# Four output projection tiles of eight by Strassen's block products in a two-layer hybrid decoder trunk

## The chip, the cores and the metric

The kernel runs on one core of a Trainium2 chip. The core has five engines that run programs of their own and meet at semaphores: TensorE (PE in the profile; its weight loads are listed as PEld), VectorE (DVE), ScalarE (ACT), GpSimd (POOL) and SyncE (SP), which issues nearly all DMAs here. Every engine takes its instructions in order. Matmuls read SBUF and write PSUM, of which this kernel uses eight banks of 128 x 512 float32. The metric is the time of one execution on the device in microseconds, median of the runs shown.

## The reference

512 tokens and 16 meta tokens in front of them (528 columns) pass through two layers with a residual stream of 1024 features, all float32. Cut to what matters:

```
for l in range(2):
    h = rmsnorm(h_res, norm_gain[l])
    u_pool, z_pool, c_q, c_kv, k_rope, z_mla, g_pool, g_mla = split(h @ w_in[l])
    y_pool = (pool_mix(u_pool, ...) * pool_scale * silu(z_pool)) @ pool_w_up[l]
    o_mla  = mla(c_q, c_kv, k_rope, ...)               # latent attention, 8 heads
    y_mla  = (o_mla * silu(z_mla)) @ mla_w_up[l]
    merged = sigmoid(g_pool) * y_pool + sigmoid(g_mla) * y_mla
    h_res  = h_res + merged @ w_out[l]                 # 1024 x 1024
return h_res[:, 16:]
```

The change is in the last line of the loop, `merged @ w_out[l]`.

## The kernel before

**Layout.** Activations lie transposed: a tile is 128 features by 528 tokens. In the second layer most work, and the output projection with it, is for the 512 real tokens alone (`self.x0` is 0 in the first layer, 16 in the last).

**Matmuls.** Each float32 operand is split into a high part, rounded to the type of the fast matmul, and a low part, the rest. `mm3` (L180) issues three matmuls: high weight by high data (L181), high weight by low data (L182), low weight by high data (L183). The weight of a step is 128 x 512 (four blocks of 128 in the contraction) and comes through `wload`: SyncE loads `raw`, ScalarE copies it to the high part `whi` (L176), VectorE subtracts to get the low part `wlo` (L177). Loads run four steps ahead of use. Data is split the same way by `split` (L274): ScalarE writes the high part (L275), VectorE the low one (L276).

**Order.** All large products stand in one list, `plan`, which the generator `stream` walks; between its steps the program of the layer (`go`) places the attention and the elementwise work. `upto` advances the stream to a named product, `fill_now` by some time of an internal clock, `after` puts a function off by such a time, and `flush` runs all that was put off. A scheduler then orders each engine's instructions by its own estimate, so the order on an engine differs from the order in the text where two instructions don't depend on each other.

**Around the change.** After the gates come the eight products `mu0` to `mu7` (contraction 512). For each, `ev_mu` multiplies the PSUM result by the gate on VectorE (L980), adds the pooled branch `am` on GpSimd into the scratch buffer `tmp` (L982; `am` is held in `xb`), and splits the sum into `mg[m]` (the names `hh` and `hl` in the profile, since the tiles lie in the buffers of the normalised input). Then come the eight output tiles `o0` to `o7`, contraction 1024, two weights each. In the first layer a tile is two halves of 264 columns, 48 matmuls of 264; in the second one half of 512, 24 matmuls, except `o7`, which has two of 256. In the first layer, where `o0` and `o1` begin, the stream puts the first weight of `o1` ahead of the second of `o0`. `ev_o` adds half of the PSUM result to the residual on VectorE (L996; the factor belongs to the gates) and stores it: to `scr` in the first layer, where the new residual stays in `xb` too and is squared and split for the next layer (L342), to the output `yT` in the second.

**Buffers.** `tmp` has three buffers, `raw` three, `whi` and `wlo` three each, the spare pair `th` and `tl` two each. PSUM has four banks `mm`, three `S` and one `o`.

Of the kernel before, what the change touches and what calls it, by code (L numbers as in the profile page):

```python
# [9 lines left out]
F32 = mybir.dt.float32  # L10
F32R = mybir.dt.float32r
# [44 lines left out]
SPL = 240  # L56
RET = 12500.0
WARM = 8


def cut(v, bits):
# [10 lines left out]
def trunk(ctx, tc, xT, xrow, mrow, pos, win, wkr, wqb, wkb, wvb, wgr, wpu, wmu, wout, gains, const, yT):  # L72
# [89 lines left out]
    class Gemm:  # L162
        def __init__(self, name, src, width, evac=None, xs=None, segs=None, body=None):
            self.name, self.src, self.width, self.alloc = name, src, width, mmt
            self.evac, self.xs, self.segs, self.body = evac, xs, segs, body
            self.spare = False

    loads = [0]

    def wload(src, n, spare):  # L170
        raw = early.pop(0) if early else fetch(src, n, rawt(), sp)
        loads[0] += 1
        pool, th, tl, nb = (tp, "th", "tl", 2) if loads[0] <= 2 or spare else (wp, "whi", "wlo", 3)
        hi = pool.tile([P, W if pool is tp else 512], F32R, tag=th, name=nm("whi"), bufs=nb)
        lo = pool.tile([P, W if pool is tp else 512], F32R, tag=tl, name=nm("wlo"), bufs=nb)
        act.activation(hi[:, :n], raw[:, :n], AF.Copy)  # L176
        dve.tensor_sub(lo[:, :n], raw[:, :n], hi[:, :n].bitcast(F32))  # L177
        return hi, lo

    def mm3(out, wh, wl, xh, xl, start, stop):  # L180
        first = pe.matmul(out, wh, xh, start=start, stop=False)  # L181
# [8 lines left out]
    def stream():  # L190
        flat = [(g_, c) for g_ in plan for c in range(0, g_.width, 512)]
        names = [g_.name for g_, c in flat]
        for i in (1, names.index((0, "o0")) + 1):
            flat[i], flat[i + 1] = flat[i + 1], flat[i]

        def load(i):
            g_, c = flat[i]
            n = min(512, g_.width - c)
# [48 lines left out]
    def after(ns, fn):  # L247
        pend.append((clk[0] + ns, fn))
        pend.sort(key=lambda e: e[0])
# [19 lines left out]
    def fill_now(ns):  # L269
        end = clk[0] + ns  # L270
        while clk[0] < end and step():
            pass

    def split(hi, lo, src, a, b):  # L274
        act.activation(hi[:, a:b], src, AF.Copy)  # L275
        return dve.tensor_sub(lo[:, a:b], src, hi[:, a:b].bitcast(F32))  # L276
# [40 lines left out]
    class Layer:  # L317
        def __init__(self, l):
            self.l, self.last = l, l == DEPTH - 1
            self.XS = XTOK if self.last else FULL  # L320
            self.x0 = NM if self.last else 0
            self.xt = xt if l == 0 else [None] * 8
            self.hs, self.us, self.zps = hbuf, [None] * 4, [None] * 4
            self.cs, self.cqs, self.ys, self.am = [None] * 2, [None] * 6, [None] * 4, [None] * 8
            self.kn, self.qn, self.zms, self.ogs = [None] * 4, [None] * 4, [None] * 4, [None] * 4
            self.qr, self.qf = [None] * 2, [None] * 2
            self.gms, self.mg, self.xr, self.vw = [None] * 8, [None] * 8, [None] * 8, []
            self.made = [None] * 8
            self.csq, self.xsq = [None] * 2, [None] * 8
            self.sq = []  # L330
            self.hosted = self.st = self.acc = self.inv = self.cinv = self.kraw = self.kp = None

        def g(self, c):
            return gn[:, self.l * N_GAIN + c:self.l * N_GAIN + c + 1]
# [640 lines left out]
        def ev_mu(self, m):  # L975
            def ev(ps, a, b):
                if a == self.x0:
                    self.mg[m] = self.hs[m]
                t = tmp()
                dve.scalar_tensor_tensor(out=t[:, :b - a], in0=self.gms[m][:, a:b], scalar=1.0, in1=ps,  # L980
                                         op0=ALU.add, op1=ALU.mult)
                gp.tensor_add(t[:, :b - a], t[:, :b - a], self.am[m][:, a:b])  # L982
# [24 lines left out]
        def register(self, nxt):  # L1007
# [4 lines left out]
            def add(name, src, width, **kw):  # L1012
                plan.append(Gemm((l, name), src, width, **kw))
# [59 lines left out]
        def go(self, nxt):  # L1073
# [58 lines left out]
            if not self.last:  # L1132
                for p in range(4):
                    self.meta_out(p)
            up("o7")
            if nxt is not None:
                for k in range(8):
# [79 lines left out]
```

## Time and profile before

| | |
|---|---|
| median of 3 runs | 770.41 us (770.23 to 770.59) |
| profiled execution, span from the first to the last instruction | 768.5 us |
| TensorE busy | 763.8 us, 99% |
| VectorE busy | 544.1 us, 71% |
| ScalarE busy | 408.9 us, 53% |
| GpSimd busy | 201.6 us, 26% |
| granted TensorE clock | 1.00 |

The profile is of one execution; what the runs' time has beyond its span, 1.9 us, lies before the first and after the last instruction. A row of the timeline gives the start in us from the span's start, the duration in us, the engine, the line of the kernel, the operation, output and inputs by the program's names, and shapes; `xN` joins N of them in a row. A row of groups gives, after the count, the union of busy time in us, the mean duration of one in ns, and the idle time of the engine ahead of them with what ended it. Durations of neighbouring instructions overlap, since each begins while the one before drains; what one costs on an engine that is full is the distance of their starts. A wait for several semaphores is put down to the one that came last.

### The profile page before, as it was taken

The page shows a single profiled execution, that of the slowest core. Times are in us where ns is not written, and L with a number is a line of the kernel's source. Part 1 is how long each engine was busy: PE and PEld are TensorE (multiplying, and loading weights), DVE is VectorE, ACT ScalarE, POOL GpSimd, SP SyncE. Part 2 cuts the span into 40 slices and gives each one's busy share as a digit, 9 for nine tenths or more (in the row PEclk, how much of TensorE's full clock was granted, in tenths as well). Part 3 has the DMA queues.
Part 4 walks back from the last instruction along what each step waited for, and adds up shares of the span by engine and source line. Part 5 has one row for each costly group of instructions (what it writes and reads, how often), then busy time and mean ns, then how long its engine had stood idle before and what let it go on. Part 6 is the DMA issues. An engine that isn't in the chain of part 4 may idle for free.

```text
span 768.5 us, 14355 instructions
## 1 busy us (share of the span) xinstructions
PE 763.8 (99%) x5195; PEld 697.9 (91%) x5195; DVE 544.1 (71%) x1179; ACT 408.9 (53%) x892; POOL 201.6 (26%) x251
## 2 busy tenths in 40 slices
PE   9999999999999999999999999999999999999998
PEld 9999999999999999999997898887888888888887
DVE  5588687357899977785376486773677989775842
ACT  6755656545556665634264355454446666664320
POOL 2026204012242233052220262040132434420500
PEclk9999999999999999999999999999999999999999
DMA  8533233343223222325642333334433332222372
GB/s 293 160 113 98 75 97 98 104 141 105 89 79 91 84 71 70 107 71 169 178 133 97 110 86 89 96 87 127 125 119 90 94 93 77 82 69 70 119 222 98
DMA packets 54931, 84.05 MB, mean 109 GB/s; under 512 B 10006, under 2 KB 18582, under 8 KB 54860
## 3 DMA queue, kind: packets, MB, share of 16 engines
q1 hardware_dynamic: 54716, 82.87, 35.6%
q8 instruction: 41, 0.67, 0.4%
q14 instruction: 30, 0.25, 0.1%
q10 hardware_dynamic: 144, 0.26, 0.1%
HBM read 76.69 MB, written 4.29 MB: 105 GB/s over the span
## 4 chain that ended last, share of the span: by engine, by line
PE 99%; DMA 0%; ACT 0%; DVE 0%; SPq 0%; issue 0%; ACTq 0%
PE mm L181 29%; PE mm L183 29%; PE mm L182 29%; PE mm L859 2%; PE S L181 2%; PE S L182 2%; PE S L183 2%; PE o L876 1%; PE o L872 1%; PE S L503 1%; PE S L470 0%; DMA xb<-xT 0%; PE S L806 0%; PE mm L922 0%; PE mm L395 0%; PE S L872 0%
## 5 line engine op out<-in xcount | busy, mean ns | idle before, releaser
L181 PE MATMUL mm<-hh,whi 128*128 128x264 f32 (+2 forms) x1080 | 339.9, 317 | 0.0
L182 PE MATMUL mm<-hl,whi 128*128 128x264 f32 (+2 forms) x1080 | 338.2, 314 | 0.0
L183 PE MATMUL mm<-hh,wlo 128*128 128x264 f32 (+2 forms) x1080 | 337.1, 315 | 0.0
L177 DVE TENSOR_TENSOR wlo<-raw,whi 128x512 fp32r<-128x512 f32 (+2 forms) x251 | 186.7, 748 | 98.6 <-ACT whi L176 94.6
L176 ACT ACTIVATE whi<-raw 128x512 fp32r<-128x512 f32 (+2 forms) x251 | 150.2, 602 | 181.3 <-PE mm L182 135.3
L181 PEld LDWEIGHTS mm<-hh,whi 128*128 128x128 f32 x1080 | 202.5, 188 | 12.9 <-ACT kp L474 0.4
L182 PEld LDWEIGHTS mm<-hl,whi 128*128 128x128 f32 x1080 | 203.0, 188 | 12.2
L183 PEld LDWEIGHTS mm<-hh,wlo 128*128 128x128 f32 x1080 | 201.9, 188 | 12.2
L743 POOL TENSOR_TENSOR tmp<-kp,bc 64x528 f32<-64x528 f32 x16 | 25.6, 1600 | 123.9 <-PE mm L183 70.0
L604 POOL TENSOR_TENSOR racc<-racc,tmp 128x264 f32<-128x264 f32 (+1 forms) x15 | 14.3, 956 | 133.1 <-ACT tmp L603 133.1
L832 POOL TENSOR_TENSOR pm<-pa,rs 128x16 f32<-128x16 f32 x32 | 9.1, 285 | 126.1 <-DVE rs L827 126.1
L982 POOL TENSOR_TENSOR tmp<-tmp,xb 128x264 f32<-128x264 f32 (+1 forms) x24 | 26.9, 1138 | 56.0 <-DVE tmp L980 55.9
L774 DVE CUSTOM_DVE_ANT_0 S<-S,maskw,nqs 128x400 f32<-128x400 f32 (+4 forms) x80 | 38.4, 499 | 4.4 <-PE S L183 4.0
L781 ACT ACTIVATE cq<-S,bia 128x400 f32<-128x400 f32 (+2 forms) x48 | 24.6, 516 | 27.1 <-DVE bia L774 18.1
L181 PE MATMUL mm<-u,whi 128*128 128x264 f32 (+1 forms) x108 | 34.7, 322 | 0.0
L181 PE MATMUL mm<-cq,whi 128*128 128x264 f32 (+1 forms) x108 | 34.7, 321 | 0.0
L183 PE MATMUL mm<-u,wlo 128*128 128x264 f32 (+1 forms) x108 | 34.7, 321 | 0.0
L183 PE MATMUL mm<-cq,wlo 128*128 128x264 f32 (+1 forms) x108 | 34.5, 321 | 0.0
L182 PE MATMUL mm<-cq,whi 128*128 128x264 f32 (+1 forms) x108 | 34.5, 321 | 0.0
L834 POOL TENSOR_TENSOR cq<-cq,rs 128x384 f32<-128x384 f32 (+1 forms) x32 | 32.8, 1024 | 0.0
L276 DVE TENSOR_TENSOR tl<-mm,th 128x384 fp32r<-128x384 f32 (+1 forms) x48 | 27.9, 596 | 5.0 <-ACT th L275 4.8
L275 ACT ACTIVATE th<-mm 128x384 fp32r<-128x384 f32 (+1 forms) x48 | 24.1, 523 | 10.2 <-PE mm L859 9.2
(270 smaller groups left out, 1378.6 us busy)
## 6 DMA issues: line engine op xcount, KB each, us to landing
raw<-win SPq DMA_DIRECT2D x143, 256.0 KB, 2.6
raw<-wout SPq DMA_DIRECT2D x32, 256.0 KB, 3.0
bc<-kdr SPq DMA_DIRECT2D x16, 264.0 KB, 3.6
raw<-wpu SPq DMA_DIRECT2D x16, 256.0 KB, 2.7
raw<-wmu SPq DMA_DIRECT2D x16, 256.0 KB, 2.7
raw<-wqb SPq DMA_DIRECT2D x12, 256.0 KB, 2.6
xb<-xT SPq DMA_DIRECT2D x8, 264.0 KB, 5.7
tmp<-xT SPq DMA_DIRECT2D x16, 132.0 KB, 3.4
```

Source lines behind the costliest of these rows:

```text
L176: act.activation(hi[:, :n], raw[:, :n], AF.Copy)
L177: dve.tensor_sub(lo[:, :n], raw[:, :n], hi[:, :n].bitcast(F32))
L181: first = pe.matmul(out, wh, xh, start=start, stop=False)
L182: pe.matmul(out, wh, xl, start=False, stop=False)
L183: newest[0] = pe.matmul(out, wl, xh, start=False, stop=stop)
L275: act.activation(hi[:, a:b], src, AF.Copy)
L276: return dve.tensor_sub(lo[:, a:b], src, hi[:, a:b].bitcast(F32))
L743: gp.tensor_mul(kf[r0:r0 + 64, :], self.kp[r0:r0 + 64, :], bc[r0:r0 + 64, :])]
L774: return dve.tensor_tensor_reduce(out=sv, in0=sv, in1=mask, scale=nqs[:, i, h:h + 1], scalar=3e38, op0=ALU.add, op1=ALU.min, accum_out=bia ...
L781: act.activation(pv, sv, AF.Exp, scale=-1.0, bias=bia[:, i:i + 1], accum_out=rs[:, c:c + 1])
L834: gp.tensor_mul(pt[i][:, NM:], pt[i][:, NM:], rs[:, i:i + 1].to_broadcast([P, n - NM]))
L982: gp.tensor_add(t[:, :b - a], t[:, :b - a], self.am[m][:, a:b])
```

## The change

`o4` to `o7` become two pairs, (4, 5) and (6, 7). A pair is a product of a 256 x 1024 weight with 1024 x 528 (or 512) data. Cut in halves in all three directions it is a 2 x 2 block product: eight block products in the plain way, seven in Strassen's (here in Winograd's form). A block product is 12 matmuls: four blocks of 128 in the contraction, three matmuls each, over half the tokens (`HV`: 264 columns in the first layer, 256 in the second).

- **Sums of data.** With `lo` and `hi` the `merged` values of the feature tiles 0 to 3 and 4 to 7, and a and b the two halves of the tokens, `combine` makes four sums for each of four tiles on VectorE: `lo_a - lo_b`, that `+ hi_b`, `hi_b - lo_b`, and the second `- hi_a`. The first and third kind follow `ev_mu` by `LAG`, the others come in `combine_split`, which splits each sum into high (ScalarE) and low (VectorE), at a distance of `PACE` after `mu7`. To keep the unsplit values, GpSimd's addition in `ev_mu` now writes `am` itself in place of `tmp`.
- **Sums of weights.** `weight_sums` loads the four 128 x 512 weights of a pair into free buffers by SyncE, each behind the newest matmul at that place, and GpSimd adds: s1 = a21 + a22, s2 = s1 + a11, a21 becomes a11 + a21, and, when the fourth operand is asked for, a12 becomes s2 + a12. (All are sums since the second tile of a pair is computed with its sign turned, which the factor -0.5 at the residual turns back.) The loads are the same in number and size as before, but bypass `raw` and its three buffers.
- **Products.** `pair_body` runs the seven. Three PSUM banks are used, and sums over products are formed in PSUM: a bank goes on accumulating after VectorE has added its state at that time to the residual (`add`, with factor 0.5 or -0.5). So VectorE reads a bank seven times per pair, and products 2, 4 and 6 follow on a bank that was just read. The residual rows of both tiles are loaded whole at the start.
- `wload`'s splitting becomes `parts`, which the pairs use on the seven weight operands (seven splits per pair where four loads were split before).
- In the second layer `o7` loses its own two halves, since the pairs have halves anyway.

```diff
+PAIRS = (2, 3)
+PACE = 300.0
...
-                gp.tensor_add(t[:, :b - a], t[:, :b - a], self.am[m][:, a:b])
-                split(*self.mg[m], t[:, :b - a], a, b)
+                f = self.am[m][:, a:b]
+                gp.tensor_add(f, t[:, :b - a], f)
+                split(*self.mg[m], f, a, b)
+                if b == T:
+                    after(LAG, lambda: self.combine(1 if m < 4 else 3, m % 4))
...
+        def combine(self, w, k):
+            f = self.tf[w, k] = sqt()[:, :n]
+            if w == 1:
+                eng.tensor_sub(f, lo[:, a0:b0], lo[:, a1:b1])
+            elif w == 2:
+                eng.tensor_add(f, hi[:, a1:b1], self.tf[1, k])
+            elif w == 3:
+                eng.tensor_sub(f, hi[:, a1:b1], lo[:, a1:b1])
+            else:
+                eng.tensor_sub(f, self.tf[2, k], hi[:, a0:b0])
+
+        def combine_split(self, w, k):
+            if w in (2, 4):
+                self.combine(w, k)
...
+            sign = -1.0 if w == 2 else 1.0
+            act.activation(th, f, AF.Copy, scale=sign)
+            dve.scalar_tensor_tensor(out=tl, in0=f, scalar=sign, in1=th.bitcast(F32), op0=ALU.mult, op1=ALU.subtract)
+
+        def weight_sums(self, p):
...
+                behind(sp.dma_start(t[m, c], wout[self.l, 2 * p + m, :, c:c + 512]), newest[0])
+            self.ws[p] = [a11, a12, s2, s1, a21, a12, a22]
+            for d, x, y in ((s1, a21, a22), (s2, s1, a11), (a21, a11, a21)):
+                fill_now(LAG if p > PAIRS[0] else 300)
+                gp.tensor_add(d, x, y)
+
+        def pair_operand(self, p):
+            def operand(i):
+                if i == 3:
+                    gp.tensor_add(ops[1], ops[2], ops[1])
+                return parts(ops[i], 512, i % 2 == 1, dve)
...
+                if i == 0:
+                    product(B, w, quarter(0, a0, b0), True)
+                    add(m1, a0, b0, B, 0.5, False)
+                elif i == 1:
+                    product(A, w, quarter(4, a0, b0), True)
+                    add(m1, a0, b0, A, 0.5, True)
+                elif i == 2:
+                    product(B, w, ts(2), False)
+                    add(m1, a1, b1, B, 0.5, False)
+                elif i == 3:
+                    product(C, w, ts(1), True)
+                    add(m2, a1, b1, C, -0.5, False)
+                elif i == 4:
+                    product(B, w, ts(3), False)
+                    add(m2, a1, b1, B, -0.5, True)
+                elif i == 5:
+                    product(C, w, quarter(4, a1, b1), False)
+                    add(m1, a1, b1, C, 0.5, True)
+                else:
+                    product(B, w, ts(4), False)
+                    add(m2, a0, b0, B, -0.5, True)
...
-            for m in range(8):
-                add(f"o{m}", wout[l, m], D, evac=self.ev_o(m, nxt), xs=mg,
-                    segs=[(NM, NM + SEQ // 2), (NM + SEQ // 2, T)] if self.last and m == 7 else XS)
+            for m in range(2 * PAIRS[0]):
+                add(f"o{m}", wout[l, m], D, evac=self.ev_o(m, nxt), xs=mg, segs=XS)
...
+            for p in PAIRS:
+                add(f"o{2 * p + 1}", None, 7 * 512, body=self.pair_body(p, nxt))
+                plan[-1].operand = self.pair_operand(p)
...
+            up("mu7")
+            flush()
+            self.weight_sums(PAIRS[0])
+            for w in (2, 1, 3, 4):
+                for k in range(4):
+                    fill_now(PACE)
+                    self.combine_split(w, k)
+            for p in PAIRS[1:]:
+                self.weight_sums(p)
             up("o7")
```

More of the change, by code (lines that the diff above doesn't have):

```diff
@@ L165, in __init__, with parts @@
             self.evac, self.xs, self.segs, self.body = evac, xs, segs, body
-            self.spare = False
+            self.spare, self.operand = False, None
     loads = [0]
+    def parts(raw, n, spare, eng):
+        pool, th, tl, nb = (tp, "th", "tl", 2) if spare else (wp, "whi", "wlo", 3)
+        hi = pool.tile([P, W if pool is tp else 512], F32R, tag=th, name=nm("whi"), bufs=nb)
+        lo = pool.tile([P, W if pool is tp else 512], F32R, tag=tl, name=nm("wlo"), bufs=nb)
+        act.activation(hi[:, :n], raw[:, :n], AF.Copy)
+        eng.tensor_sub(lo[:, :n], raw[:, :n], hi[:, :n].bitcast(F32))
+        return hi, lo
     def wload(src, n, spare):
@@ L172, in wload @@
         loads[0] += 1
[L173 to L178, printed above, removed]
+        return parts(raw, n, loads[0] <= 2 or spare, dve)
     def mm3(out, wh, wl, xh, xl, start, stop):
@@ L197, in load @@
             g_, c = flat[i]
+            if g_.operand is not None:
+                return g_.operand(c // 512)
             n = min(512, g_.width - c)
@@ L331, in __init__ @@
             self.hosted = self.st = self.acc = self.inv = self.cinv = self.kraw = self.kp = None
+            n = (T - self.x0) // 2
+            self.HV = [(self.x0, self.x0 + n), (self.x0 + n, T)]
+            self.tf, self.ts, self.ws = {}, {}, {}
         def g(self, c):
@@ new lines, in weight_sums @@
+        def weight_sums(self, p):
+            tags = (("cq0", "cq1", "cq2", "cq3", "kn0", "kn1"), ("q0", "q1", "q2", "q3", "kn2", "racc"))[p % 2]
+            t = {}
+            for tag, (m, c) in zip(tags, ((0, 0), (0, 512), (1, 0), (1, 512))):
+                t[m, c] = slot(tag)[:, 0:512]
+                behind(sp.dma_start(t[m, c], wout[self.l, 2 * p + m, :, c:c + 512]), newest[0])
+            a11, a12, a21, a22 = (t[k] for k in ((0, 0), (0, 512), (1, 0), (1, 512)))
+            s1, s2 = (slot(tag)[:, 0:512] for tag in tags[4:])
+            self.ws[p] = [a11, a12, s2, s1, a21, a12, a22]
+            for d, x, y in ((s1, a21, a22), (s2, s1, a11), (a21, a11, a21)):
+                fill_now(LAG if p > PAIRS[0] else 300)
+                gp.tensor_add(d, x, y)
@@ L1134, in go @@
                     self.meta_out(p)
+            up("mu7")
+            flush()
+            self.weight_sums(PAIRS[0])
+            for w in (2, 1, 3, 4):
+                for k in range(4):
+                    fill_now(PACE)
+                    self.combine_split(w, k)
+            for p in PAIRS[1:]:
+                self.weight_sums(p)
             up("o7")
```

51 lines of the change are left out of this document (added).

## The prediction

> **What bounds the kernel now.** First the page's busy times and the chain of work that ended last:
>
> ```profile
> PE 763.8 (99%) x5195; PEld 697.9 (91%) x5195; DVE 544.1 (71%) x1179; ACT 408.9 (53%) x892; POOL 201.6 (26%) x251
> PE 99%; DMA 0%; ACT 0%; DVE 0%; SPq 0%; issue 0%; ACTq 0%
> ```
>
> TensorE is busy for 763.8 of 768.5 us, and 99% of the chain is TensorE: a matmul fewer is time won, as long as nothing makes TensorE wait. So the question is what a matmul costs, and how close the other engines already are where the change adds work to them. Prices of matmuls, from the timeline of TensorE (start, duration; the durations overlap, the pace is start to start):
>
> ```profile
> 351.93 0.28 PE L181 MATMUL mm<-hh,whi 128*128 128x264 f32 x1
> 353.39 0.28 PE L181 MATMUL mm<-hh,whi 128*128 128x264 f32 x1
> 730.83 0.39 PE L181 MATMUL mm<-hh,whi 128*128 128x512 f32 x1
> 737.76 0.39 PE L181 MATMUL mm<-hh,whi 128*128 128x512 f32 x1
> 759.25 0.28 PE L181 MATMUL mm<-hh,whi 128*128 128x256 f32 x1
> 760.67 0.28 PE L181 MATMUL mm<-hh,whi 128*128 128x256 f32 x1
> ```
>
> The first two rows are 12 matmuls apart, the next two 30, the last two 12: 0.122 us for 264 columns, 0.231 for 512, 0.118 for 256.
>
> Next the stretch in which the `mu` tiles are evicted, just ahead of the output projection, once per layer (columns: span of the stretch, then busy us of PE, PEld, DVE, ACT, POOL):
>
> ```profile
> 329.42:351.63 22.21, 22.21 (x184) 22.21 (x183) 20.73 (x38) 10.54 (x23) 14.58 (x16) 1.00 0.27 78
> 708.07:728.55 20.48, 20.48 (x90) 16.57 (x89) 19.38 (x24) 9.56 (x16) 12.29 (x8) 1.00 0.30 92
> 731.00:765.00 34.00, 34.00 (x171) 28.52 (x170) 11.65 (x19) 6.32 (x10) 0.00 (x0) 1.00 0.53 164
> ```
>
> VectorE's 71% is a mean. In both `mu` stretches it is at 93 to 95%, while in the projection itself it is at a third. The groups of those two stretches (count, busy us, mean ns, idle before) show what it does there:
>
> ```profile
> L276 DVE TENSOR_TENSOR hl<-tmp,hh 128x264 fp32r<-128x264 f32 x16 | 11.3, 720 | 1.2 <-ACT hh L275 1.2
> L177 DVE TENSOR_TENSOR wlo<-raw,whi 128x512 fp32r<-128x512 f32 x6 | 4.8, 819 | 0.0
> L980 DVE SCALAR_TENSOR_TENSOR tmp<-cq,mm 128x264 f32<-128x264 f32 x12 | 4.8, 421 | 3.2 <-PE mm L183 3.0
> ...
> L177 DVE TENSOR_TENSOR wlo<-raw,whi 128x512 fp32r<-128x512 f32 x8 | 8.8, 1117 | 0.0
> L276 DVE TENSOR_TENSOR hl<-tmp,hh 128x512 fp32r<-128x512 f32 x8 | 7.1, 905 | 1.1 <-ACT hh L275 1.1
> ```
>
> The subtraction L276 has the same width as the eviction L980, and takes 720 ns to its 421. The timeline says why:
>
> ```profile
> 343.40 0.76 DVE L980 SCALAR_TENSOR_TENSOR tmp<-cq,S 128x264 f32<-128x264 f32 x2
> 343.96 2.58 POOL L982 TENSOR_TENSOR tmp<-tmp,xb 128x264 f32<-128x264 f32 x3 [1.12 <-DVE tmp L980]
> 344.08 0.93 DVE L276 TENSOR_TENSOR hl<-tmp,hh 128x264 fp32r<-128x264 f32 x1
> ```
>
> Two evictions take 0.76 us together, 0.34 from one to the next; a subtraction that begins while GpSimd adds needs 0.93 alone. Operations with two SBUF inputs wait for GpSimd's and the other way round; those that read PSUM don't. So VectorE and GpSimd together are nearly full here.
>
> **What is saved.** Per layer the change replaces four tiles by 2 x 7 products of 12 matmuls, 168 in all. In the first layer they replace 192 of the same width: 24 x 0.122 = 2.9 us. In the second they are 256 wide and replace three tiles of 24 at 512 and one of 48 at 256: 72 x 0.231 + 48 x 0.118 - 168 x 0.118 = 2.5. Together 5.4 us, all on the path.
>
> **What is added to VectorE.** Per layer 16 token sums and 16 splits of a half row (0.34 each; the 256 columns of the second layer are priced the same), 14 evictions for 8 (for 5 in layer two), and the weight splits 14 for 8. In the projection this has room. But in the changed kernel's order on VectorE, 12 sums and 7 splits of them stand ahead of the last split of `mg7`, which every output tile needs: 19 x 0.34 = 6.5 us. Nothing shows that they hide: they have two SBUF inputs, like L276. They can use the idle time that the groups show, 1.2 and 1.1.
>
> First layer: `mg7` is split here:
>
> ```profile
> 351.20 0.43 DVE L276 TENSOR_TENSOR hl<-tmp,hh 128x264 fp32r<-128x264 f32 x1 [0.20 <-ACT hh L275]
> 354.62 0.29 PE L182 MATMUL mm<-hl,whi 128*128 128x264 f32 x1
> ```
>
> It ends at 351.63 and TensorE reads it at 354.62, a margin of 3.0. TensorE's order up to that matmul holds the same work in both kernels, so it waits 6.5 - 1.2 - 3.0 = 2.3 us. After that VectorE has 3 weight splits (0.6 each) and 9 short ones up to the low part of `o2`'s first weights, 4.9 us, against 41 matmuls, 5.0: the wait neither grows nor shrinks.
>
> Second layer: the last split ends at 728.55, and here one more weight split stands ahead of it (0.6), so it comes 6.5 + 0.6 - 1.1 = 6.0 later, at 734.5:
>
> ```profile
> 727.87 0.68 DVE L276 TENSOR_TENSOR hl<-tmp,hh 128x512 fp32r<-128x512 f32 x1
> 720.38 0.39 PE L181 MATMUL mm<-hh,whi 128*128 128x512 f32 x1
> ```
>
> TensorE begins `o0` at 720.38 and has 46 matmuls of 512 and 10 of 256 (part of the first product, moved up) before it needs it: 720.4 + 10.6 + 1.2 = 732.2, a wait of 2.4. Then VectorE has 3 weight splits, 10 short ones and two evictions (3 x 0.6 + 10 x 0.34 + 2 x 0.6 = 6.4) up to the low part of `o2`'s second weights, TensorE only 20 matmuls (4.4): 2.0 more, 4.4 in all.
>
> **GpSimd's sums of weights**, four per pair, 512 wide. The nearest row of that width that nobody holds up:
>
> ```profile
> L604 POOL TENSOR_TENSOR racc<-racc,tmp 128x512 f32<-128x512 f32 x5 | 6.5, 1292 | 68.4 <-ACT tmp L603 68.4
> ```
>
> Three of them, 3.9 us, follow the `mu` additions directly, so they fall on those late splits of VectorE. If they land beside evictions or waits they cost 0, if they hold VectorE up for their whole time 3.9 per layer; I take the middle, 2.0 and 1.9. The Trainium skill (SBUF — State Buffer, "Who interferes with whom") says that the shared pair of ports is held for the whole instruction and the other engine blocks fully: by that it would be the upper end, and the time about 3.9 us more than I forecast; the 0.93 us row agrees with the rule, but not that every sum must meet a split.
>
> **Loads and banks.** The parts' weights are as many loads as before, but in the second layer SyncE's order has pair 3's four behind a store of `yT` that waits for pair 2's first finished half.
>
> ```profile
> raw<-wout SPq DMA_DIRECT2D x32, 256.0 KB, 3.0
> 764.81 0.28 PE L183 MATMUL mm<-hh,wlo 128*128 128x256 f32 x1
> 765.13 0.42 DVE L996 SCALAR_TENSOR_TENSOR tmp<-mm,tmp 128x256 f32<-128x256 f32 x1 [0.99 <-PE mm L183]
> ```
>
> Some 3 us for the first and perhaps 1 each for the others (an estimate), then up to four sums of 1.3 and a split: 13 us, against the 105 matmuls of 256, 12.4 us, that stand between; only the operand made last is that late. Bounds 0 and 2, I take 0.5. Products of one bank follow each other with other work between, except the last two of the second layer: there TensorE waits from its last start (764.81 in the old end) until the eviction is over, 0.7 us. The residual rows and stores are the same bytes. ScalarE gets 16 short copies and 6 weight copies more per layer; at 10.5 of 22 us it has room, so I take 0. The end (a 256-wide eviction and its store) stays.
>
> **Sum.** -5.4 + (2.3 + 2.0) + (4.4 + 1.9) + 0.5 + 0.7 = +6.4 us, made on an execution of 768.5 us span; the runs' median is 770.4, 1.9 more, which the change leaves as it is. Forecast 776.8. With no GpSimd hold and no late load: -5.4 + 2.3 + 4.4 + 0.7 = +2.0, 772.4. With both whole: -5.4 + 6.2 + 8.3 + 2.7 = +11.8, 782.2.
>
> **Rivals.** (1) Faster: the lateness hides. Of VectorE's time 16 x (720 - 420) + 6 x (819 - 680) ns = 5.6 us in the first stretch is waiting for GpSimd (680 is a 512-wide subtraction unhindered, the 727.87 row), in the second 8 x 437 + 8 x 225 = 5.3. The change lets GpSimd write its sum in place, which frees the three `tmp` buffers sooner; if GpSimd then runs beside the evictions, 5.6 + 1.2 pays for 6.5. It decides when VectorE regains some 5 us per layer. Then only the bank wait is left: 765.7. Against it: GpSimd needs some 0.86 us for each of 16 additions (2.58 for the three above) and the 16 evictions offer 0.34 of cover each. Chance 0.17. (2) Half of that: waits about equal the saving, 769 to 772.3, chance 0.09; 0.2% (1.5 us) is about what a measurement of this kernel can tell from no change, and 0.08 lies within it. (3) The clock. Every stretch above has a granted clock of 1.00, with no wait of microseconds in it; the new waits are the first. Were the clock halved for some 3.4 us after each of the two, 1.7 us each would be lost: 780.2, chance 0.08. The Trainium skill (TensorE: Matmul & The Clock Gate, "What's actually happening") has that rule, half rate after an idle window of about 3.4 us; no run so far shows it, and the waits are broken up by matmuls. The forecast itself has 0.66.
>
> **The range** 765.6 to 782.5 holds rival 1's value and the upper bound; some 0.08 lies below and 0.08 above. The forecast's own range is 772.4 to 782.2. Faster 0.17, the same 0.08, slower 0.75.
>
> **What would show it.** In the new profile: TensorE idle by some microseconds between the last `mu` tile and `o2` in both layers, released by VectorE (`hl`, then `wlo`); VectorE over 95% there; 264- and 256-wide products at 0.122 and 0.118; the new sums at 0.7 or more where GpSimd runs; no idle time inside the products except the last bank. I am wrong if TensorE stays gapless at `mg7`: then rival 1 holds and 5 us are gained.

## The result, and the profile after

The changed kernel takes 796.16 us (median of 4 runs, 794.90 to 797.41) against 770.5 for the kernel before on the same chip: a ratio of 1.0333, 95% interval 1.0318 to 1.0348. It is slower by 25.7 us; the forecast was 776.8 with a range to 782.5. The profiled execution took 797.41 us with a span of 795.6, 27.1 more than the span before.

The busy times and the chain of the changed kernel:

```profile
PE 771.6 (97%) x5219; PEld 703.6 (88%) x5219; DVE 591.0 (74%) x1270; ACT 426.5 (54%) x936; POOL 223.6 (28%) x267
...
PE 88%; DVE 7%; DMA 2%; issue 1%; POOL 0%; ACT 0%; SPq 0%; DVEq 0%; ACTq 0%
```

Before, 99% of the chain was TensorE; now 7% of the way to the end runs over VectorE and 2% over transfers. What TensorE waits for in the whole execution, the six largest rows (total us, times, longest):

```profile
PE mm L187 <- DVE hl L283: 5.5, 4, 2.9
PE mm L1062 <- DVE tmp L1068: 3.9, 3, 3.0
PE mm L1062 <- ACT whi L176: 2.8, 1, 2.8
PE mm L186 <- DVE tmp L990: 2.1, 2, 1.9
PE S L1062 <- ACT whi L176: 1.5, 2, 0.9
PE S L1062 <- DVE wlo L177: 1.4, 1, 1.4
```

Line 283 is `mg`'s split, 990 the eviction of the `mu` tiles, 1068 the eviction of the products, 176 and 177 the split of weights. None of these rows stood in the old profile. Where they lie, in stretches of 5 us (columns: us; busy time of TensorE, its weight loads, VectorE, ScalarE and GpSimd with instruction counts; granted clock; DMA share; GB/s):

```profile
345.00:350.00 5.00, 4.01 (x33) 3.80 (x31) 5.00 (x10) 2.02 (x6) 2.55 (x3) 1.00 0.17 62
350.00:355.00 5.00, 4.05 (x20) 4.05 (x21) 5.00 (x11) 1.80 (x5) 2.63 (x3) 0.66 0.31 91
355.00:360.00 5.00, 5.00 (x43) 5.00 (x42) 5.00 (x10) 3.29 (x8) 2.50 (x4) 1.00 0.75 255
360.00:365.00 5.00, 2.10 (x17) 1.88 (x16) 5.00 (x7) 2.31 (x5) 3.63 (x3) 1.00 0.01 2
...
380.00:385.00 5.00, 4.10 (x33) 3.76 (x31) 1.88 (x3) 1.69 (x3) 3.24 (x3) 1.00 0.83 267
385.00:390.00 5.00, 2.52 (x18) 2.35 (x19) 4.35 (x9) 2.32 (x4) 4.11 (x3) 1.00 0.63 187
...
740.00:745.00 5.00, 3.11 (x12) 1.64 (x10) 5.00 (x5) 2.71 (x6) 3.72 (x4) 1.00 0.71 236
745.00:750.00 5.00, 2.76 (x10) 2.06 (x11) 5.00 (x8) 1.86 (x6) 2.96 (x2) 0.74 0.00 0
750.00:755.00 5.00, 5.00 (x17) 4.19 (x16) 5.00 (x14) 2.94 (x8) 0.00 (x0) 0.58 0.19 52
...
770.00:775.00 5.00, 2.29 (x20) 2.08 (x18) 0.42 (x1) 0.54 (x1) 0.00 (x0) 0.97 0.78 233
775.00:780.00 5.00, 4.24 (x18) 3.95 (x19) 2.21 (x5) 1.42 (x4) 2.67 (x3) 0.50 0.48 157
```

Three things are to be seen. VectorE is busy the whole time from 345 to 365 and from 740 to 755 while TensorE is not. At 380 to 390 and 770 to 775 VectorE is not full and the DMA engines are busy for 0.63 to 0.83 of the time: these waits are for transfers, as the rows below show. And behind several stops the clock column drops (0.66, 0.74 and 0.58, 0.50): TensorE is busy and slow.

The 27.1 us, from the trace: for every matmul the time to the start of the next, less the usual one of its shape, added up by place.

| term | forecast | measured |
|---|---|---|
| saving of the products | -5.4 | -5.5 |
| first layer, `mu` to `o2` | 2.3 + 2.0 | 6.1 of waits (2.10, 3.06, 0.97), 1.6 of slow clock |
| first layer, residual rows of the pairs | 0 | 3.7 (3.13, 0.57) |
| second layer, `mu` to `o3` | 4.4 + 1.9 | 6.3 of waits (seven, the longest 1.93), 3.2 of slow clock |
| second layer, pair 3's loads | 0.5 | 5.0 of waits (3.01 the longest), 2.3 of slow clock |
| last bank | 0.7 | 0.7 |
| the start | 0 | 1.9 |
| the tail, and gaps under 0.3 | 0 | 1.8 |

The start: in the stretch from 5 to 10 us TensorE got 36 matmuls done before and 21 in the changed kernel's profiled execution, although the granted clock is shown as 1.00 in both. From 5.98 to 9.94 its matmuls start at twice their usual spacing, which costs 1.86 us.

```profile
5.00:10.00 5.00, 4.91 (x36) 4.68 (x37) 4.02 (x8) 3.55 (x7) 0.00 (x0) 1.00 0.99 317
```

```profile
5.00:10.00 5.00, 4.81 (x21) 4.69 (x22) 3.40 (x7) 3.50 (x7) 0.00 (x0) 1.00 0.94 307
```

The first row is of the kernel before, the second of the changed one. The four runs of the changed kernel fall into two pairs 2.3 us apart; the profile is of the upper pair.

**The first layer's stop at 360.** The timeline of the changed kernel has VectorE's four sums of line 1008 (two SBUF inputs) beside GpSimd's first weight sum:

```profile
357.98 3.63 DVE L1008 TENSOR_TENSOR sq<-xb,sq 128x264 f32<-128x264 f32 x4
...
358.45 1.45 POOL L1037 TENSOR_TENSOR kn<-cq,cq 128x512 f32<-128x512 f32 x1 [1.72 <-DMA cq<-wout]
```

Four sums take 3.63 us; at 0.34 from one to the next they would take 1.4. The first eviction of `mu0` and the last split of `mg7` are these:

```profile
331.34 1.11 DVE L990 SCALAR_TENSOR_TENSOR tmp<-cq,mm 128x264 f32<-128x264 f32 x3 [2.92 <-PE mm L188]
...
362.97 0.42 DVE L283 TENSOR_TENSOR hl<-xb,hh 128x264 fp32r<-128x264 f32 x1
```

The split ends 32.05 us after the eviction began, in the kernel before 22.21: 9.8 us later. 6.5 of it is the price of the 19 new operations, and 3.3 come from GpSimd's three weight sums, as the run without them shows below; none of the old idle time came back. TensorE had a margin of 3.0 us, so it must come 6.8 us late to that split, and it does: 2.10 us of stop at a `mu` eviction, 1.6 of slow clock and 3.06 of stop at the split. The slow clock adds nothing here: at full speed TensorE would have stood 1.6 us longer at the split.

**The residual rows.** The longest wait of VectorE from 370 to 392:

```profile
DVE xb L1126 <- DMA tmp<-xT: 4.9, 2, 4.4
```

And SyncE's issues in that time (start us, us, line, transfer):

```profile
374.91 1.43 SPq L1031 DMA_DIRECT2D q<-wout  x3
376.38 0.45 SPq L1123 DMA_DIRECT2D tmp<-xT  x1
...
377.35 2.04 SPq L1123 DMA_DIRECT2D tmp<-xT  x2
...
382.76 0.38 SPq L1086 DMA_DIRECT2D tmp<-xT  x1
...
385.69 0.38 SPq L1086 DMA_DIRECT2D tmp<-xT  x1
```

The rows of the last output tile (line 1123) are issued behind pair 3's weight loads (line 1031) and share the transfers with them; VectorE stands 4.4 us at that tile's eviction. The pair's own rows (line 1086) go into `tmp`, which has three buffers, and each waits for such an eviction and its store to free one. So the first product's eviction has its row only after 386, and TensorE waits for the bank.

**Pair 3's loads.** The chain from 765 to 777 (start us, us, what):

```profile
765.98 2.98 DMA yT<-tmp
...
768.97 0.32 SPq L1086
...
769.82 0.42 SPq L1031
...
770.29 5.55 DMA q<-wout
...
775.87 0.64 ACT whi L176
```

SyncE cannot issue the load of a residual row (line 1086) until a store has freed its `tmp` buffer, and pair 3's four weight loads (line 1031) stand behind it in SyncE's order. They are issued from 769.82 on, when pair 2 has some 2 us of matmuls left. The first weight has landed at 774.36, behind the stop of 3.01 us, and the second, 5.55 us under way, at 775.84, behind the stop of 0.91.

### The profile page after: what moved, and what is told of

Same layout as the page of the kernel before. It is cut to its first block, busy times and chain, and to the rows that moved or that the text cites. A ratio compares the mean times of both kernels' runs of the same rounds, so it can differ in the third digit from the quotient of the medians.

```text
span 795.6 us, 14545 instructions
## 1 busy us (share of the span) xinstructions
PE 771.6 (97%) x5219; PEld 703.6 (88%) x5219; DVE 591.0 (74%) x1270; ACT 426.5 (54%) x936; POOL 223.6 (28%) x267
## 4 chain that ended last, share of the span: by engine, by line
PE 88%; DVE 7%; DMA 2%; issue 1%; POOL 0%; ACT 0%; SPq 0%; DVEq 0%; ACTq 0%
PE mm L186 24%; PE mm L188 24%; PE mm L187 24%; PE mm L1062 3%; PE mm L869 2%; DVE wlo L177 2%; PE S L186 2%; PE S L188 2%; PE S L187 2%; DVE hl L283 1%; PE o L886 1%; PE o L882 1%; DVE tmp L990 1%; DMA tmp<-xT 1%; PE S L513 1%
## 5 line engine op out<-in xcount | busy, mean ns | idle before, releaser
L187 PE MATMUL mm<-hl,whi 128*128 128x264 f32 (+1 forms) x976 | 308.8, 317 | 5.5 <-DVE hl L283 5.5
L186 PE MATMUL mm<-hh,whi 128*128 128x264 f32 (+1 forms) x976 | 309.8, 319 | 2.1 <-DVE tmp L990 2.1
L188 PE MATMUL mm<-hh,wlo 128*128 128x264 f32 (+1 forms) x976 | 306.7, 318 | 0.0
L177 DVE TENSOR_TENSOR wlo<-raw,whi 128x512 fp32r<-128x512 f32 (+2 forms) x235 | 175.8, 751 | 79.1 <-ACT whi L176 75.4
L176 ACT ACTIVATE whi<-raw 128x512 fp32r<-128x512 f32 (+2 forms) x235 | 140.0, 600 | 142.5 <-PE mm L187 92.2
L187 PEld LDWEIGHTS mm<-hl,whi 128*128 128x128 f32 x976 | 185.1, 190 | 18.2 <-DVE hl L283 7.4
L186 PEld LDWEIGHTS mm<-hh,whi 128*128 128x128 f32 x976 | 184.8, 190 | 14.4 <-DVE tmp L990 2.8
L188 PEld LDWEIGHTS mm<-hh,wlo 128*128 128x128 f32 x976 | 184.0, 190 | 11.6 <-DVE wlo L177 0.6
L993 POOL TENSOR_TENSOR xb<-tmp,xb 128x264 f32<-128x264 f32 (+1 forms) x24 | 26.8, 1137 | 63.2 <-DVE tmp L990 63.2
```

Source lines behind the costliest of these rows:

```text
L177: eng.tensor_sub(lo[:, :n], raw[:, :n], hi[:, :n].bitcast(F32))
L187: pe.matmul(out, wh, xl, start=False, stop=False)
L188: newest[0] = pe.matmul(out, wl, xh, start=False, stop=stop)
L993: gp.tensor_add(f, t[:, :b - a], f)
```

## The experiments

Theory A, after the trace: the products save what was forecast, and the loss is made of four things that can be taken away one by one: data sums on VectorE ahead of `mg7`, GpSimd's weight sums that hold VectorE up, transfers issued late, and the slow clock behind every stop. Theory B: VectorE, GpSimd and the loads are simply too full there, so what is moved comes back elsewhere.

**No data sums.** The `after(LAG, combine)` and the splits are gone, and the products read quarters of `mg` in their place.

```diff
-                if b == T:
-                    after(LAG, lambda: self.combine(1 if m < 4 else 3, m % 4))
...
-                ts = lambda w_: [self.ts[w_, k] for k in range(4)]
+                ts = lambda w_: quarter(4 * (w_ % 2), a0, b0)
...
-                    self.combine_split(w, k)
```

> The data sums and their splits are left out (the three products that read them read quarters of the merged data in their place, so the output is not the reference's); all matmuls, weight sums, loads and stores stay. Theory A (VectorE's sums and splits ahead of mg7, made longer by GpSimd's weight sums, are the largest cause: 17.4 of the 27 us in the profile of the changed kernel, waits of 13 us and 4 to 5 us of slow clock after them): the waits between the last mu tile and o2 are gone in both layers, what stays is the late residual rows (3.7) and the late loads of pair 3 (some 7), about 777 us. Rival B (GpSimd's weight sums alone hold VectorE up): the waits at mg7 stay, about 790. Rival C (the transfers are the cause of everything, the waits at mg7 only pass time that would be lost anyway): 790 or more.

Measured: 777.48 us, ratio 1.0095 (1.0079 to 1.0112). The waits for `mg7` are gone in both layers, and with them every stretch of slow clock behind the start; the longest wait left is 1.9 us. The time is the one expected, but not its make-up: of pair 3's loads, which were to keep some 7 us, only waits of up to 0.8 us are left, and small waits elsewhere make up the rest.

**No weight sums.** GpSimd's four additions per pair are left out; unsummed blocks stand in their place.

```diff
             for d, x, y in ((s1, a21, a22), (s2, s1, a11), (a21, a11, a21)):
                 fill_now(LAG if p > PAIRS[0] else 300)
-                gp.tensor_add(d, x, y)
...
-                if i == 3:
-                    gp.tensor_add(ops[1], ops[2], ops[1])
```

> GpSimd's sums of weights are left out (the products read plain weights in their place, so the output is not the reference's); data sums, splits, matmuls, loads and stores stay. Theory A with the port held whole by each weight sum: of mg7's 9.8 us of lateness in the first layer 3.0 go and 1.1 at o2's weights, about as much in the second, so 8 to 10 us less, about 786 us, with a wait of 2 to 5 us left at mg7 in both layers. Rival B: mg7 on time, about 778. If GpSimd's sums cost nothing (rival D, they run beside evictions): 795 as it is.

Measured: 782.73 us, ratio 1.0153 (1.0138 to 1.0168), between the 786 of theory A and the 778 of rival B. Sixteen additions of 1.3 to 1.8 us on an engine that is 28% busy cost 13.4 us of the time. The same four sums of line 1008, in the groups of VectorE from 352 to 362 of this run:

```profile
L1008 DVE TENSOR_TENSOR sq<-xb,sq 128x264 f32<-128x264 f32 x4 | 1.4, 418 | 0.0
```

418 ns each and not 964: the difference is GpSimd's. The first eviction and the last split of the first layer:

```profile
329.46 1.11 DVE L990 SCALAR_TENSOR_TENSOR tmp<-cq,mm 128x264 f32<-128x264 f32 x3 [3.12 <-PE mm L188]
...
357.81 0.42 DVE L283 TENSOR_TENSOR hl<-xb,hh 128x264 fp32r<-128x264 f32 x1
```

They lie 28.77 us apart, 6.6 more than in the kernel before and 3.3 less than in the changed kernel, whose three weight sums take 4.3 us there. In the second layer the distance falls from 32.06 to 28.32 us. The first layer's wait for `mg7`'s last split is gone: the stop at the `mu` eviction (2.07) and the slow clock behind it (1.6) have used up the lateness. A wait of 0.94 us that is left there is for a weight's split on ScalarE (line 176). Pair 3's wait (2.91) stays.

**Everything late.** All sums ordered behind `mg7`'s last split, residual rows in `xb`, both pairs' eight weight loads issued at once behind `mu7`. Some of the sums then read values that the first layer's evictions have overwritten in `xb`.

```diff
-                if b == T:
-                    after(LAG, lambda: self.combine(1 if m < 4 else 3, m % 4))
...
+            follow(ins, self.low)
...
-                        st["x", m] = tmp()
+                        st["x", m] = xb[:, m]
...
+            for p in PAIRS:
+                self.weight_loads(p)
```

> All data sums are ordered behind the last split of mg7, the residual rows of the pairs are loaded into xb in place of the three tmp buffers, and the weights of both pairs are loaded as soon as mu7 is done. Nothing is left out. Theory A with late transfers as the second cause: the waits at mg7 go, VectorE makes the 32 sums and splits while o0 to o3 run; it needs about 26 us with GpSimd's sums for 22 to 23 us of matmuls, so 0 to 4 us of wait may stay per layer: 766 to 772 us. If the sums cost the same wherever they stand (rival C): 785 or more.

Measured: 790.5 us, ratio 1.026 (1.0245 to 1.0275), far from the 766 to 772 expected. What TensorE waits for:

```profile
PE mm L186 <- ACT whi L176: 7.2, 1, 7.2
PE mm L188 <- DVE wlo L177: 3.4, 1, 3.4
PE S L188 <- DVE wlo L177: 2.8, 1, 2.8
```

The second and third row are the first layer's splits of weights of the output tiles, now behind the block of sums. The 7.2 us lie in the second layer, from 744.7 to 752.0, and come from ScalarE's order:

```profile
747.50 0.42 ACT L1022 ACTIVATE kl<-sq 128x256 fp32r<-128x256 f32 x1 [2.39 <-DVE sq L1006]
...
751.36 0.61 ACT L176 ACTIVATE whi<-raw 128x512 fp32r<-128x512 f32 x1
```

The last ordinary weight load ahead of them had landed at 741.78, but its split (line 176) stands behind splits of data sums (line 1022), which wait for VectorE's sums. The waits moved, as theory B has it; but they moved to what had been put in the way, so this run alone does not tell the theories apart.

**Stops of known length.** The kernel before, with TensorE held at `o1`, `o3`, `o5` and `o7` by one to four chained GpSimd additions.

```diff
+    STOP = {"o1": 1, "o3": 2, "o5": 3, "o7": 4}
...
+                                last = gp.tensor_add(d[:, 0:512], d[:, 0:512] if j else cst_src[0], cst_src[0])
...
+                            behind(made, last)
```

> The kernel before, with TensorE made to wait for 1, 2, 3 and 4 chained GpSimd additions of 128x512 (1.3 us each) at the start of o1, o3, o5 and o7 of both layers, the order of the output tiles' matmuls fixed. Theory clock (an idle stretch of about 3.4 us or one that covers a whole window of the monitor halves the clock): after the stops of 1.3 and 2.6 us the pace stays at 0.122 and 0.231 us, after 3.9 and 5.2 us some 3.4 us run at double these. Rival (the clock stays at full speed and the slow matmuls of the changed kernel have another cause): the pace is the same after all stops.

Measured: 818.82 us, in a single run. Four stretches of it:

```profile
350.00:355.00 5.00, 2.56 (x11) 2.56 (x12) 2.33 (x4) 1.36 (x3) 2.39 (x3) 0.69 0.46 139
...
370.00:375.00 5.00, 3.48 (x19) 3.48 (x20) 0.34 (x1) 0.00 (x0) 1.46 (x1) 0.74 0.40 124
...
390.00:395.00 5.00, 5.00 (x33) 5.00 (x32) 0.45 (x1) 0.63 (x1) 0.00 (x0) 0.71 0.00 0
...
405.00:410.00 5.00, 1.72 (x8) 1.72 (x9) 0.00 (x0) 0.00 (x0) 3.07 (x3) 0.65 0.17 52
```

In the first layer the stops cost 2.87, 3.06, 4.34 and 5.74 us, and behind each the matmuls start at twice their spacing for 2.6 to 4.8 us, 1.38, 1.65, 1.61 and 2.33 us more. It is the same in the second layer (1.4 to 2.2 us). A stop of less than the 3.4 us of rival 3 is enough, which was not expected; so that rival was a real effect. In the changed kernel a slow stretch follows the stops of 2.10 and 3.01 us and the row of stops about 746, but not those of 3.06 and 3.13 in the first layer. In the changed kernel and the runs made from it there are 13 stops of 2 us or more after the start; nine have a slow stretch within 2 us behind them, four (2.07, 2.60, 3.06 and 3.13 us) have none. What decides between these is open.

**Transfers alone.** All sums stay; the pairs' residual rows go to `xb`, and pair 3's weight loads are issued in the middle of the data splits. The rows land while later sums still read there, so those sums see other values.

```diff
-                        st["x", m] = tmp()
+                        st["x", m] = xb[:, m]
...
+                if w == 1:
+                    for p in PAIRS[1:]:
+                        self.weight_loads(p)
```

> All sums stay where the change puts them; only transfers move: the residual rows of the pairs land in rows of xb instead of tmp buffers, and pair 3's four weight loads are issued in the middle of the splits of the data sums. Theory A (these transfers were late for want of a buffer and of a place in SyncE's queue): the two waits at layer 0's residual rows (3.13 and 0.57 us) and, in layer 1, pair 3's wait of 3.01 and 0.91 us with the 2.3 us of half clock behind it and the 0.84 us after it go: 796.2 - 3.7 - 7.1 = about 785.4. Theory B (VectorE and GpSimd are that far behind that the pairs would wait anyway): 792 or more, the same waits put down to VectorE.

Measured: 786.24 us, ratio 1.0204 (1.0189 to 1.0219); 785.4 was expected of theory A, 792 of B. The wait for the residual rows and pair 3's wait are gone, with the slow clock behind it. 9.9 us of the loss go when the transfers are in a better place. The three removals so far (18.7, 13.4 and 9.9 us) add up to 42.0, more than the 31.2 there are (25.7 and the 5.5 saved): they overlap, and none of them is a share of the loss.

**The products alone.** No sums of either kind, transfers as in the last run: the edits of the runs above together.

> The seven products alone: no data sums and no weight sums are made (the products read quarters of the data and unsummed weights, so the output is not the reference's), and the transfers are placed as in e4b_transfers. Theory A (the products save what they were priced at, all of the loss lies in the sums and loads): 770.4 - 5.4 + 0.7 at the last bank = 765.7, with no wait over 1 us behind mu0. Theory B (half-width products and their interleaved groups cost TensorE something themselves): 768 or more.

Measured: 772.98 us, ratio 1.0029 (1.0015 to 1.0044), runs from 770.5 to 776.3. Its matmuls of 264 and 256 columns keep their 0.122 and 0.118 us (by such prices all matmuls take 745.14 us, against 750.61 before), but the gain is not seen. The waits in its profile:

```profile
PE mm L1062 <- DVE xb L1068: 2.5, 2, 1.9
...
PE mm L1062 <- ACT hh L350: 1.0, 1, 1.0
PE mm L187 <- DVE hl L352: 0.8, 1, 0.8
```

So theory A falls in its form that all of the loss lies in the sums and the loads. A product lasts 1.46 us and its bank is wanted again a product or two later, where an output tile of the first layer lasts 5.9 (48 x 0.122): the products tolerate little lateness of an eviction. The 1.9 us wait at 377, with 1.5 us of slow clock behind it, comes while GpSimd adds squares for the next layer (375.57 to 378.61); two of VectorE's weight splits take 1.40 and 1.45 us beside it, and 0.68 later. The last runs test this cause. The two rows below it lie at the end of the first layer's pairs, where the second layer begins.

**Weight sums early.** Nothing is left out. The sums of weights are made on GpSimd behind the last head, beside the `gm` products, in buffers that attention has left, and kept to the pairs; raw blocks come through the ordinary weight loads. Four data sums stay beside `mu`, the others follow `mg7`'s split; residual rows in `xb`.

```diff
+            tags = ("kh", "kl", "kh", "kl") if p == PAIRS[0] else ("q4", "q5", "q6", "q7") if self.last else ("cq8", "cq9", "cq10", "cq11")
...
+            self.sums += [(a22, a21), (a21, a11), (a11, a22), (a12, a11)]
...
+                d, x = self.sums.pop(0)
+                follow(gp.tensor_add(d, d, x), self.pmul)
```

> The same seven products for both pairs of both layers, with the whole result: the eight weight sums of a layer are made on GpSimd behind the last head, beside the gm products, into buffers that attention has left; only the first four data sums are made beside the mu products, the other twelve behind the last split of mg7, the splits spread to where the products need them; residual rows go to xb. Theory A (the loss was place, not work): all waits at mg7 and of pair 3's loads go, 766 to 769. Theory B (VectorE's added 11 us don't fit beside the first output tiles wherever they are put): waits of 1 to 3 us at o0 to o2, each with half clock behind it, 772 to 780.

Measured: 775.63 us, ratio 1.0058 (1.0042 to 1.0075): 20 us better than the changed kernel with all of its arithmetic, but not the 766 to 769 of theory A; it is in theory B's 772 to 780.

```profile
PE mm L188 <- DVE wlo L177: 3.5, 4, 1.6
PE mm L1068 <- DVE xb L1074: 2.8, 3, 1.8
```

The splits of `o0`'s and `o1`'s weights stand behind a block of twelve sums and eight splits on VectorE.

**One pair a layer**, otherwise the same: `PAIRS = (3,)`.

> As e10_weight_sums_early with one pair (o6 and o7) a layer: four weight sums, the same sixteen data sums and splits, now beside six output tiles in place of four, half the saving. Theory A: 770.4 - 2.7 + 0.4 = about 768. Theory B (the data sums alone are too much beside mu7 and o0): 771 or more.

Measured: 776.39 us, ratio 1.0075 (1.006 to 1.009), theory B's side again. The same waits at `o0` and `o1`, since the data sums are the same sixteen.

**VectorE's work spread evenly.** From the first layer's twelfth sum on, each sum and split waits for a matmul beside which it is to run; the square of `o3` was moved in the program too.

```diff
+            for what, w, ns in ((self.combine, 3, 100.0), (self.combine, 2, 600.0), (self.combine_split, 2, 800.0),
+                                (self.combine, 4, 700.0), (self.combine_split, 1, 1200.0), (self.combine_split, 3, 1200.0),
+                                (self.combine_split, 4, 1300.0)):
+                for k in range(4):
+                    what(w, k)
+                    pace(ns)
...
+            behind(ins, newest[0])
```

> e10_weight_sums_early with VectorE's added work held to TensorE's progress: four data sums at mg7, then each further sum and split waits for the matmul beside which it is to run, and layer 0's square sums of o3 on GpSimd are put behind the pairs. Whole result. Theory A (only the order on VectorE was left): e10_weight_sums_early's waits of 1.48 us at o0, 1.95 us with 1.61 us of half clock at the first pair of layer 0, and 3.32 us at o0 and o1 of layer 1 go, and its run started 2.1 us later than the run of before: 776.3 - 8.4 - 2.1 = about 766, its span some 2 to 4 us under the span of before. Theory B (there is no room for it): no better than 773.

> The same with one pair a layer: half of the 5.4 us saved, the same sixteen data sums, four weight sums. Theory A: about 768.5. Theory B: 772 or more.

Measured: 775.24 us with two pairs (1.0058, 1.0046 to 1.007; its profiled run 773.66, span 771.9) and 772.51 with one (1.0028, 1.002 to 1.0037). Both miss theory A's numbers (766 and 768.5) and meet theory B's. The first layer's waits at `o0` are gone, the second layer's halved. The wait in the first pair stayed, 2.6 us now, and the trace shows what it lies beside:

```profile
375.14 3.10 POOL L360 TENSOR_TENSOR cq<-cq,cq 128x528 f32<-128x528 f32 x2 [9.91 <-ACT cq L356]
...
375.62 1.45 DVE L177 TENSOR_TENSOR wlo<-raw,whi 128x512 fp32r<-128x512 f32 x1
...
377.00 1.54 DVE L1028 SCALAR_TENSOR_TENSOR bc<-sq,bc 128x264 fp32r<-128x264 f32 x1
```

GpSimd adds two squares of rows (line 360) from 375.14 to 378.24, and beside them VectorE needs 1.45 and 1.54 us for operations that take 0.68 and 0.42. The square had been moved in the program, but nothing made it wait, and the scheduler put it back.

**The last two corrections.** That square now waits for a matmul of the pairs, and the second layer's data sums all begin 4 us after `mu7`.

```diff
             made = act.activation(self.xsq[k][:, :T], self.xt[k][:, :T], AF.Square)
+            behind(made, newest[0])
...
+            if self.last:
+                pace(4000.0)
```

> e12_even with two corrections of place: layer 0's square of o3 and the GpSimd sums behind it now wait for a matmul of the pairs, and layer 1's data sums all begin 4 us after mu7 instead of beside the mu products. Whole result. Theory A (what was left of e12_even's waits, 2.60 and 0.74 us at layer 0's first pair and 2.3 us at o0 and o1 of layer 1, was order alone): 4 to 5 us less, a span of about 767 against 768.5 before, 769 in the runs. Theory B (VectorE is full): the waits come back elsewhere, 773 or more.

> The same corrections with one pair a layer. Theory A: the 2.3 us at o0 and o1 of layer 1 go, 772.5 - 2.3 = about 770, level with before or 0.1% under it. Theory B: 772 or more.

Measured with two pairs: 772.22 us, ratio 1.0014 (1.0004 to 1.0023). The profiled run took 769.78 with a span of 768.0; its waits are

```profile
PE S L1070 <- ACT whi L176: 1.4, 1, 1.4
PE mm L1070 <- DVE xb L1076: 1.1, 2, 0.6
...
PE mm L1070 <- DVE wlo L177: 0.5, 1, 0.5
```

and no stretch of slow clock beyond the start. Of 5.5 us saved in pace 5.2 are given back around the projection, 3.7 of them in four waits. The runs spread from 769.8 to 773.2 and the profile is of the fastest; what the others lose is not known. With one pair: 769.57 us, ratio 0.9985 (0.9977 to 0.9994), runs from 769.37 to 769.90. That is 1.1 us (0.15%) less than the kernel before beside it (770.65), and as theory A expected. Its only wait in the pairs is the last bank's:

```profile
PE mm L1070 <- DVE xb L1076: 0.5, 1, 0.5
```

The wait at the square sums went from 2.6 to 0.7 us, and in that layer the squares were all that moved, which settles its cause. Theory A holds for most of the loss: with all the arithmetic kept, 24 of the 25.7 us went by place and order alone. Its forecasts of a gain with two pairs all failed: no order tried there came under the kernel before. One pair keeps 1.1 of the 2.8 us that its matmuls save.

## Why the prediction was wrong

- **The saving** (-5.4) was right: -5.5, and the pace of the products as priced.
- **The last bank** (0.7) was right: 0.68.
- **`mg7` in the first layer** (2.3 + 2.0): the mechanism was right, the size not, 7.7. The lateness was 9.8 us and not 6.5 - 1.2 + 2.0 = 7.3. The step that took 1.2 us of idle time off failed, none came back: without weight sums the lateness was 6.6. The middle taken for GpSimd failed too: its sums held VectorE up for 3.3 us, nearer to the upper bound of 3.9 than to 2.0. The last 1.0 us is the next wait, at 365: the prediction let the lateness neither grow nor shrink there, but the weight split that ends it took 1.80 us beside GpSimd's fourth sum. The Trainium skill (SBUF — State Buffer, "Who interferes with whom") lets a VectorE instruction with two SBUF inputs contend with a GpSimd instruction that reads SBUF. The trace agrees, with 964 against 418 ns. The prediction named the rule and the bound and chose the middle on the ground that not every sum must meet a split; here VectorE ran without a pause, and the sums met it for most of their time.
- **A stop not foreseen** was that of 2.10 us at 348.7, for an eviction of a `mu` tile (line 990): the prediction followed the lateness only to `mg7`'s split, but the `mu` evictions stand in the same queue. It moved part of the wait to an earlier place and did not add to it.
- **`mg7` in the second layer** (4.4 + 1.9): the same, 6.3 of waits and 3.2 of slow clock. The last split came 11.6 us late, where 6.0 + 1.9 were forecast; all four weight sums of the first pair (5.9 us on GpSimd) ran ahead of it, and without them it came 7.8 late.
- **The slow clock** was a rival with a chance of 0.08 and should have been a term. The slow matmuls behind the new stops took 7.1 us more than usual, but that is not all loss: the first layer's 1.6 were hidden by the wait for VectorE, and how much of the other 5.5 would have been waited anyway is open. The Trainium skill (TensorE: Matmul & The Clock Gate, "What's actually happening") gives half rate after at least one idle window of about 3.4 us, and by it none of the changed kernel's stops (3.13 at most) would have been long enough. The traces disagree on the length, and agree on half rate, here for 3.7 to 4.7 us.
- **"The residual rows and stores are the same bytes"** failed: 3.7 us. The bytes are the same; their place is not, behind pair 3's weight loads in SyncE's order and in `tmp` buffers that must first come free. Pair 3's loads were priced in the second layer alone, and in the first they delayed these rows. The run that moved rows and loads alone took these waits away, and 9.9 us in both layers together.
- **Pair 3's late loads** (0.5, bounds 0 and 2) failed in size: 7.3 us. The place was seen, SyncE's order behind a `yT` store. But the price was made of a load's 3 us and the others' 1 each against 12.4 us of matmuls, as if the issue came in time; the loads were issued 2 us before the pair was over, and the first two then took 4.5 and 5.55.
- **The start**, 1.9 us in the profiled execution, was in no term; nothing shows that the change has a part in it.

No single term did it: of the 20.7 us between the forecast for the span (774.9) and the span, by place some 10.5 lie at the transfers, 3.4 and 3.2 in the two stretches at `mg7`, 1.9 at the start, and 1.8 in the tail and small gaps.

## What to carry to other kernels

Price added work on an engine by what stands behind it in that engine's queue, all the way to TensorE, and allow for some 1.5 us of slow clock behind a stop of 2 us or more on TensorE: here it came behind nine of 13, and it costs only where TensorE would not have waited anyway. Before calling a moved transfer free, ask which buffer it takes, for how long, and what else in the issuing queue now waits for that buffer. A GpSimd addition on SBUF beside a full VectorE costs most of its time (3.3 of 4.3 us, and 3.7 of 5.9), so precomputation belongs in a stretch in which VectorE has slack: the same arithmetic took 25.7 us more than the old kernel in one place and 1.6 more in another, and half of it 1.1 less.

## What the hardware showed that was not expected

- Behind many stops of TensorE of 2 us and more, matmuls start at twice their spacing for some 2 to 5 us (0.5 to 0.74 granted in the 5 us stretches). All eight stops made with chained additions had it, the shortest 1.6 us behind smaller ones; of 13 others nine had it and four, up to 3.13 us, did not.
- The start of an execution can cost 2 us more or less: 36 or 21 matmuls in the same 5 us, those of the slower one at twice their spacing, with a granted clock of 1.00 shown for both. The runs of the two-pair versions spread over up to 6 us and those of the fastest one-pair version over 0.5; whether the start is the reason, and what sets it, was not tried.
